# A one-layer hybrid encoder on one core: three products of a constant at the start, and a planner that runs eight passes

## The chip, the cores and the metric

The kernel runs on one core of a Trainium2 chip. The time is device microseconds of one execution; the median of 3 runs of the kernel before is 2115.37 us (2114.18 to 2116.24). A difference of about 0.2% (4.2 us) is what is treated here as a change.

## The reference, cut to what matters

One layer of a streaming encoder on 1024 frames of width 1024, all in float32, with a final norm:

```
h = rmsnorm(x);  proj = h @ w_in                 # 11 groups of columns
A: gated DeltaNet (conv + SiLU, l2 norm, chunked triangular solve, scan over chunks)
B: gated linear attention (low-rank forget gate, scan over chunks)
x += (sigmoid(a) * (o_a @ w_a) + sigmoid(b) * (o_b @ w_b)) @ w_out
x += cross attention of rmsnorm(x) over 256 memory tokens (4 heads)
x += square(relu(rmsnorm(x) @ w1)) @ w2
return rmsnorm(x)
```

The first matrix work on the chip is the keys and values of the memory tokens (`wk`, `wv`), since it needs the least data.

## The kernel before

Every float32 product is made of three fast ones (`fp32r`): each operand is split into a high part (a copy on ScalarE, line 622, or line 736 for the memory tokens) and a low part (a difference, line 623 or 737), and `mm3` (lines 582, 584 and 586) multiplies high by high, high by low and low by high into one PSUM bank (`pd`, or `ps`). Weights are loaded by SP in pieces of 128x512 into `raw` tiles and split into `wop` (or `whi` and `wlo`) tiles. So TensorE needs, for each piece of weights, one load, one ScalarE row and one VectorE row. PSUM banks are emptied by ScalarE (lines 935, 1302, 1588) and VectorE (line 940).

The big projections use a seven-product scheme on 2x2 blocks: lines 1757 to 1765 form sums of weight blocks before they are split, in place in `raw`. `t`, `A0a`, `A1b`, `B0b`, `B1b` are operand tiles on the activations' side. Other names that come up: line 1275 is one tap of the convolution, line 1176 and line 654 a merge of three buffers and the transposes that read one of them, line 1437 fills `PF`, the inverted diagonal blocks of the triangular solve, with four copies of one quarter each, and line 1449 multiplies by them.

The order of the instructions is not the order of the code. The program is traced once, then a planner (`Plan`) lays it out and the program is built again in that order. The planner gives each instruction a duration out of a formula (`Op`), works out backwards when each must be done at the latest (`latest`), and then runs forward in time: each engine takes, of what is ready, the instruction with the earliest latest time (`forward`); TensorE takes the first in the program. Some sums and low parts may run on VectorE or on GpSimd (POOL); `forward` chooses for each. Latest times go back from where TensorE is expected to be. `make` repeats the two steps and keeps the layout that ends first by the planner's own account:

```
for _ in range(ROUNDS):
    start, order = self.forward(deps, self.latest(deps, at, max(at) + 5000))
    at, end = start, max(start)
    if best is None or end < best[0]:
        best = end, order, [o.eng for o in self.ops if o.flex], start
```

With `ROUNDS` 1, the expected times of TensorE's work (`at`) are a plain sum of the durations; from the second pass on they are those of the pass before, waits included. `apply` then ties each engine's instructions together in the order kept. On the chip each engine runs its queue strictly in that order, and SP issues its loads and stores so too.

The run starts with `consts`: an identity, a 128x16 tile `mhalf` filled with -0.5 (used as an exponent by POOL), a column of ones and two small loads. SP meanwhile loads the first pieces of `wk` and the memory tokens.

Of the kernel before, what the change touches and what calls it, by code (L numbers as in the profile page):

```python
# [18 lines left out]
P = 128  # L19
# [8 lines left out]
HALF = 512  # L28
# [13 lines left out]
SE = ((0, 0, 0, 0, 0, 0, 0, 0), (0, 1, 0, 1, 1, 1, 0, 1), (0, 1, 0, 1, 0, 1, 0, 0))  # L42
FJ = 12
KRAW = 4
LAYW = (("raw", 2048, 2), ("whi", 4096, 2), ("wlo", 4096, 2))
FF = ((24, 24), (24, 24))
HEAD = (0, 1, 2)
# [26 lines left out]
OUT = "out_0_dram"  # L74
HOLD, MARGIN = 0, 0
SOON = 0
ROUNDS, TOP, PAD, WINDOW, LOAD, HORIZON, LAND, RATE = 1, 228656, 128, 3413, 1283, 30000, 2600, 300
ISSUE = 400
HEADIN = ('in_memT_dram', 'in_wk_dram', 'in_wv_dram')

# [420 lines left out]
class Layer:  # L501
# [134 lines left out]
    def wpart(self, src, shape, lo_eng=None, lp=None, before=None, rp=None):  # L636

        raw = self.til(rp or self.wp, [P] + shape, "raw", bufs=RAWS if rp is None else KRAW)
        hi = self.til(self.wp, [P] + shape, "wop", F32R, bufs=RING)
# [60 lines left out]
    def consts(self):  # L700
        nc, a = self.nc, self.a
        cp = self.cp = self.pool(self.ctx, "const", "left")
        self.room(cp, 160)
        self.ident = self.til(cp, [P, P], "ident")
        make_identity(self.tc.nc, self.ident)
        self.mhalf = self.til(cp, [P, 16], "mhalf")
        nc.vector.memset(self.mhalf, -0.5)
        self.ones = self.til(cp, [P, 1], "ones")
        nc.vector.memset(self.ones, 1.0)
        cols = self.til(cp, [P, 56], "cols")  # L710
        nc.scalar.dma_start(cols, a["cols"])
        self.g_mix, self.g_x = cols[:, 0:8], cols[:, 8:16]
        self.g_mem, self.g_mlp = cols[:, 16:24], cols[:, 24:32]
        self.b_gate, self.g_fin = cols[:, 32:36], cols[:, 48:56]
        self.a_log, self.dt_bias = cols[:, 39:40], cols[:, 40:41]

        self.g_gdn, self.g_gla = cols[:, 36:37], cols[:, 37:39]
        self.convw = self.til(cp, [P, 24, 4], "convw")
        nc.sync.dma_start(self.convw, a["convw"])
        self.tm = self.til(cp, [P, NB, 2, GH], "tm")  # L720
        self.geg = self.til(cp, [P, NB, GH], "geg")
        self.gneg = self.til(cp, [P, NB, GH], "gneg")
# [846 lines left out]
    def phase_gdn(self, wp):  # L1569

        nc, a = self.nc, self.a
        with ExitStack() as ctx:
# [3 lines left out]
            self.lay(sp, LAYP)  # L1576
            self.lay(wp, LAYW)
            self.lay(sq, LAYQ)
# [891 lines left out]
```

## Time and profile before

| | |
|---|---|
| median of 3 runs | 2115.37 us |
| the profiled execution, its own time | 2115.5 us |
| its span in the profile | 2113.8 us |
| granted TensorE clock | 0.999 |
| TensorE matmul (PE), busy | 2091.5 us (99%), 10938 records |
| VectorE (DVE), busy | 1595.6 us (75%) |
| ScalarE (ACT), busy | 1208.1 us (57%) |
| GpSimd (POOL), busy | 152.2 us (7%) |
| moved by DMA | 329.57 MB, mean 156 GB/s |

The span is what lies between the first and the last instruction of the program; the execution takes 1.7 us more. PE's busy time counts overlapped matmuls once, so a short wait can hide inside it: two matmuls of 128x512 follow each other in 0.23 us while each row is 0.39 us long. In a row of the timeline the figures are the start in us, the duration in us, and in brackets the engine's idle time before it with what ended it; of a wait of n us the bracket shows what the overlap has left.

### The profile page before, as it was taken

The page shows a single profiled execution, that of the slowest core. Times are in us where ns is not written, and L with a number is a line of the kernel's source. Part 1 is how long each engine was busy: PE and PEld are TensorE (multiplying, and loading weights), DVE is VectorE, ACT ScalarE, POOL GpSimd, SP SyncE. Part 2 cuts the span into 40 slices and gives each one's busy share as a digit, 9 for nine tenths or more (in the row PEclk, how much of TensorE's full clock was granted, in tenths as well). Part 3 has the DMA queues.
Part 4 walks back from the last instruction along what each step waited for, and adds up shares of the span by engine and source line. Part 5 has one row for each costly group of instructions (what it writes and reads, how often), then busy time and mean ns, then how long its engine had stood idle before and what let it go on. Part 6 is the DMA issues. An engine that isn't in the chain of part 4 may idle for free. (4 is left out here: it accounts for less than half of the span.)

```text
span 2113.8 us, 30953 instructions
## 1 busy us (share of the span) xinstructions
PE 2091.5 (99%) x10938; PEld 1780.5 (84%) x10938; DVE 1595.6 (75%) x2830; ACT 1208.1 (57%) x2391; POOL 152.2 (7%) x174
## 2 busy tenths in 40 slices
PE   8999999999999999999999999999999999999998
PEld 8889887898888899889888888888788888888887
DVE  7858887948876888787569899469967567567855
ACT  7456666536646586765655456565755557444433
POOL 0000000001001223311000000000100000000000
PEclk9999999999999999999999999999999999999999
DMA  8322232312325444555586752226444446678852
GB/s 329 130 72 62 91 105 64 113 61 96 100 93 194 131 129 139 168 176 162 176 278 239 257 169 80 90 79 218 137 145 140 160 151 219 212 249 278 269 175 100
DMA packets 158363, 329.57 MB, mean 156 GB/s; under 512 B 17016, under 2 KB 25720, under 8 KB 158208
## 3 DMA queue, kind: packets, MB, share of 16 engines
q1 hardware_dynamic: 158064, 327.57, 47.1%
q8 instruction: 86, 1.41, 0.3%
q14 instruction: 69, 0.57, 0.1%
q10 hardware_dynamic: 144, 0.03, 0.0%
HBM read 227.36 MB, written 100.17 MB: 155 GB/s over the span
## 5 line engine op out<-in xcount | busy, mean ns | idle before, releaser
L622 ACT ACTIVATE wop<-raw 128x512 fp32r<-128x512 f32 (+1 forms) x520 | 336.6, 653 | 406.4 <-PE pd L586 179.5
L623 DVE TENSOR_TENSOR wop<-raw,wop 128x512 fp32r<-128x512 f32 (+1 forms) x494 | 347.3, 707 | 209.3 <-ACT wop L622 206.4
L582 PE MATMUL pd<-t,wop 128*128 128x512 f32 x332 | 130.4, 393 | 0.9 <-ACT t L622 0.9
L586 PE MATMUL pd<-t,wop 128*128 128x512 f32 x332 | 130.9, 394 | 0.0
L584 PE MATMUL pd<-t,wop 128*128 128x512 f32 x332 | 130.7, 394 | 0.0
L584 PE MATMUL pd<-A1b,wop 128*128 128x512 f32 x272 | 106.1, 390 | 0.0
L582 PE MATMUL pd<-A1b,wop 128*128 128x512 f32 x272 | 106.0, 390 | 0.0
L586 PE MATMUL pd<-A1b,wop 128*128 128x512 f32 x260 | 101.4, 390 | 1.4 <-DVE wop L623 1.4
L1275 DVE SCALAR_TENSOR_TENSOR dx<-dx,convw,dx 128x1023 f32<-128x1023 f32 (+2 forms) x72 | 90.3, 1277 | 2.2 <-ACT dx L1273 2.0
L582 PE MATMUL pd<-A1a,wop 128*128 128x512 f32 x208 | 81.6, 392 | 0.0
L584 PE MATMUL pd<-A1a,wop 128*128 128x512 f32 x208 | 81.5, 392 | 0.0
L586 PE MATMUL pd<-A1a,wop 128*128 128x512 f32 x196 | 76.7, 391 | 0.0
L582 PEld LDWEIGHTS pd<-t,wop 128*128 128x128 f32 x332 | 62.2, 188 | 14.5 <-ACT t L622 1.3
L584 PEld LDWEIGHTS pd<-t,wop 128*128 128x128 f32 x332 | 62.3, 188 | 13.2 <-DVE t L623 0.4
L586 PEld LDWEIGHTS pd<-t,wop 128*128 128x128 f32 x332 | 62.4, 188 | 12.8
L622 ACT ACTIVATE whi<-raw 128x512 fp32r<-128x512 f32 x70 | 43.0, 628 | 34.3 <-PE pd L584 15.2
L582 PEld LDWEIGHTS pd<-A1b,wop 128*128 128x128 f32 x272 | 51.1, 188 | 10.6 <-ACT wop L622 0.3
L584 PEld LDWEIGHTS pd<-A1b,wop 128*128 128x128 f32 x272 | 51.1, 188 | 10.4
L586 PEld LDWEIGHTS pd<-A1b,wop 128*128 128x128 f32 x260 | 48.8, 188 | 11.9 <-DVE wop L623 1.9
L623 DVE TENSOR_TENSOR wlo<-raw,whi 128x512 fp32r<-128x512 f32 x65 | 44.0, 685 | 17.7 <-ACT whi L622 17.7
L940 DVE TENSOR_TENSOR dx<-pd,dx 128x512 f32<-128x512 f32 x51 | 35.0, 687 | 16.9 <-PE pd L586 16.7
L582 PEld LDWEIGHTS pd<-A1a,wop 128*128 128x128 f32 x208 | 39.0, 188 | 8.3 <-ACT dx L935 0.3
(645 smaller groups left out, 6497.0 us busy)
## 6 DMA issues: line engine op xcount, KB each, us to landing
raw<-in_w_dram SPq DMA_DIRECT2D x120, 256.0 KB, 3.8
raw<-in_w_dram SPq DMA_DIRECT2D x32, 512.0 KB, 3.8
e<-ad SPq DMA_DIRECT2D x63, 256.0 KB, 4.7
ad<-q SPq DMA_DIRECT2D x45, 256.0 KB, 2.7
rawa<-ad SPq DMA_DIRECT2D x42, 256.0 KB, 4.6
A0b<-tgd SPq DMA_DIRECT2D x32, 256.0 KB, 5.2
ad<-acc SPq DMA_DIRECT2D x30, 256.0 KB, 2.3
ad<-u SPq DMA_DIRECT2D x30, 256.0 KB, 2.6
```

The source lines that it names most:

```text
L582: nc.tensor.matmul(out, lh, rh, start=first and i == 0, stop=False, skip_group_check=True)
L584: nc.tensor.matmul(out, lh, rl, start=False, stop=False, skip_group_check=True)
L586: nc.tensor.matmul(out, ll, rh, start=False, stop=last and i == n - 1, skip_group_check=True)
L622: nc.scalar.activation(hi, raw, AF.Copy)
L623: (lo_eng or nc.gpsimd).tensor_tensor(lo, raw, hi.bitcast(F32), SUB)
L940: nc.vector.tensor_tensor(o, pt, o, ADD)
L1275: self.nc.vector.scalar_tensor_tensor(y[:, d:], x[:, :T - d], cw[:, 3 - d:4 - d], y[:, d:], MUL, ADD)
```

## The change

Two edits. After `mhalf` is set, three products of it with itself (16 columns of weights, a moving operand of 512 columns made by repeating the tile, plain float32) go into a PSUM bank that nothing reads. And the planner makes eight passes in place of one and keeps the one that ends first by its own account.

```
+WARM = 3
...
-ROUNDS, TOP, PAD, WINDOW, LOAD, HORIZON, LAND, RATE = 1, 228656, 128, 3413, 1283, 30000, 2600, 300
+ROUNDS, TOP, PAD, WINDOW, LOAD, HORIZON, LAND, RATE = 8, 228656, 128, 3413, 1283, 30000, 2600, 300
...
         nc.vector.memset(self.mhalf, -0.5)
+        pt = self.pss()
+        half = self.mhalf.rearrange("p (a b) -> p a b", a=1).broadcast_to([P, HALF // 16, 16])
+        for _ in range(WARM):
+            nc.tensor.matmul(pt[:16], self.mhalf, half, start=True, stop=True)
         self.ones = self.til(cp, [P, 1], "ones")
```

The added line of constants moves all later lines down by one, and the four lines in `consts` those after them by four more: line 623 of the kernel before is line 624 after, line 1275 is line 1280. Every tile that is made after the added bank carries a number that is higher by 1 in its first part and by 4 in its last.

TensorE's order starts with the three products and is otherwise nearly the same row by row in its first units; the queues of the other engines are laid out anew from about 20 us on. Three places follow.

VectorE, at the end of the second group of projections (near 350 us in the trace of before). `wop_3456` is the low part of a piece of weights that TensorE waits for; the lines 1275 (1280 after) are taps of the convolution. Before:

```order
L1275 SCALAR_TENSOR_TENSOR dx_3390<-dx_3279,convw_194,dx_3390 128x1022
L1275 SCALAR_TENSOR_TENSOR dx_3410<-dx_3362,convw_194,dx_3410 128x1023
L1275 SCALAR_TENSOR_TENSOR dx_3390<-dx_3279,convw_194,dx_3390 128x1021
L1275 SCALAR_TENSOR_TENSOR dx_3410<-dx_3362,convw_194,dx_3410 128x1022
L623 TENSOR_TENSOR wop_3456<-raw_3345,wop_3456 128x512
L1275 SCALAR_TENSOR_TENSOR dx_3410<-dx_3362,convw_194,dx_3410 128x1021
L1760 TENSOR_TENSOR raw_3345<-raw_3346,raw_3345 128x4x128
L1077 SCALAR_TENSOR_TENSOR ex_3222<-ex_3214,ex_3222 128x1024
```

And after (`wop_3460` is the same piece):

```order
L1082 SCALAR_TENSOR_TENSOR ex_3226<-ex_3218,ex_3226 128x1024
L1280 SCALAR_TENSOR_TENSOR dx_3394<-dx_3283,convw_198,dx_3394 128x1023
L624 TENSOR_TENSOR wop_3460<-raw_3349,wop_3460 128x512
L1280 SCALAR_TENSOR_TENSOR dx_3394<-dx_3283,convw_198,dx_3394 128x1022
L1280 SCALAR_TENSOR_TENSOR dx_3414<-dx_3366,convw_198,dx_3414 128x1023
L1280 SCALAR_TENSOR_TENSOR dx_3394<-dx_3283,convw_198,dx_3394 128x1021
L1280 SCALAR_TENSOR_TENSOR dx_3414<-dx_3366,convw_198,dx_3414 128x1022
L1765 TENSOR_TENSOR raw_3349<-raw_3350,raw_3349 128x4x128
L1280 SCALAR_TENSOR_TENSOR dx_3414<-dx_3366,convw_198,dx_3414 128x1021
```

The low part stood behind four taps and stands ahead of them now; the long row of line 1077 (1082) moved ahead of both.

ScalarE, in the first unit of the triangular solve (near 735 us). `whi` are high parts of weights, `PF` the four copies of line 1437 (1442), `acc_...<-pd` evictions. Before:

```order
L622 ACTIVATE whi_7517<-raw_7519 128x512
L1302 ACTIVATE acc_7498<-pd_7471 128x512
L622 ACTIVATE whi_7517<-raw_7523 128x512
L1302 ACTIVATE acc_7514<-pd_7501 128x512
L622 ACTIVATE fold_7784<-raw_7782 128x512
L1437 ACTIVATE PF_6319<-X_6317 32x32x16 x4
L622 ACTIVATE whi_7787<-raw_7789 128x512
```

And after:

```order
L623 ACTIVATE whi_7521<-raw_7527 128x512
L623 ACTIVATE fold_7788<-raw_7786 128x512
L1307 ACTIVATE acc_7518<-pd_7505 128x512
L1569 ACTIVATE acc_7675<-pd_7531 128x512
L623 ACTIVATE whi_7791<-raw_7793 128x512
L623 ACTIVATE whi_7791<-raw_7797 128x512
L1442 ACTIVATE PF_6323<-X_6321 32x32x16 x3
L623 ACTIVATE whi_7821<-raw_7823 128x512
L1569 ACTIVATE acc_7783<-pd_7678 128x512
L1442 ACTIVATE PF_6323<-X_6321 32x32x16
```

Two more splits and an eviction stand ahead of the copies into `PF`, and a split and an eviction between the third copy and the fourth. On SP the load of the first of these `whi` pieces (`raw_7523` after) stands right behind two loads of 512 KB (`v`) that stood 24 and 20 rows ahead of it before.

POOL, from the output projection on (1250 to 1600 us). `u`, `raw`, `acc` are sums that `forward` may place on VectorE or on POOL. Before:

```order
L1757 TENSOR_TENSOR raw_12811<-raw_12811,raw_12812 128x4x128
L613 TENSOR_TENSOR rs_y_13287<-n_v_13285,mhalf_188 128x4
L613 TENSOR_TENSOR rs_y_13375<-n_v_13373,mhalf_188 128x4
L1711 TENSOR_TENSOR m_13923<-m_13923 128x512
L623 TENSOR_TENSOR B1b_14659<-q_14655,B1b_14659 128x512
L1762 TENSOR_TENSOR raw_15561<-raw_15561,raw_15560 128x4x128
L1757 TENSOR_TENSOR raw_15747<-raw_15747,raw_15748 128x4x128
```

And after:

```order
L1716 TENSOR_TENSOR u_12572<-u_12572,q_12305 128x512
L1762 TENSOR_TENSOR raw_12815<-raw_12815,raw_12816 128x4x128
L692 TENSOR_TENSOR acc_12619<-acc_12619,e_12728 128x512
L692 TENSOR_TENSOR acc_12619<-acc_12619,e_12979 128x512
L614 TENSOR_TENSOR rs_y_13291<-n_v_13289,mhalf_188 128x4
L614 TENSOR_TENSOR rs_y_13379<-n_v_13377,mhalf_188 128x4
L1762 TENSOR_TENSOR raw_14341<-raw_14341,raw_14342 128x4x128
L1765 TENSOR_TENSOR raw_14670<-raw_14671,raw_14670 128x4x128
L1767 TENSOR_TENSOR raw_15565<-raw_15565,raw_15564 128x4x128
L1762 TENSOR_TENSOR raw_15751<-raw_15751,raw_15752 128x4x128
L624 TENSOR_TENSOR wop_15737<-raw_15564,wop_15737 128x512
```

The low part of `B1b` left POOL for VectorE; where one large sum stood at the start of the stretch (the first row) there are four now, one behind the other, and in all of the stretch nine where there were five.

## The prediction

> **What bounds the kernel now.** I read the page's busy shares first, then the list of TensorE's waits, then the timeline around each wait.
>
> ```profile
> PE 2091.5 (99%) x10938; PEld 1780.5 (84%) x10938; DVE 1595.6 (75%) x2830; ACT 1208.1 (57%) x2391; POOL 152.2 (7%) x174
> PE pd L582 <- ACT mT L736: 6.2, 2, 5.5
> PE pd L582 <- ACT q L935: 1.9, 2, 1.7
> PE pd L586 <- DVE wlo L623: 1.8, 2, 1.2
> PE ps L654 <- DVE ex L1176: 1.6, 1, 1.6
> PE pd L586 <- DVE wop L623: 1.4, 1, 1.4
> PE pd L582 <- ACT t L622: 0.9, 1, 0.9
> PE ps L1369 <- DVE kdt L1345: 0.4, 1, 0.4
> 2105.69 0.39 PE L586 MATMUL ps<-wop,A1b 128*128 128x512 f32 x1
> 2110.78 0.33 SPq L2250 DMA_DIRECT2D out_dram<-B0b  x1
> ```
>
> TensorE is the bound. It idles 6.2 us before and among its first products, 8.0 us in eight shorter waits (1.9 + 1.8 + 1.6 + 1.4 + 0.9 + 0.4), and 8 us behind its last matmul, which the change leaves as they are. All that a new order can win is in those 14 us and in the pace of the start; what it can lose has no such limit.
>
> The start shows a second loss, in stretches of the windows view and two pairs of matmuls:
>
> ```profile
> 5.50:8.10 2.60, 1.96 (x7) 1.64 (x7) 1.58 (x3) 1.69 (x5) 0.00 (x0) 1.00 1.02 321
> 8.10:11.50 3.40, 3.32 (x15) 3.32 (x16) 3.31 (x8) 3.40 (x10) 0.00 (x0) 1.00 1.04 368
> 11.50:14.90 3.40, 3.40 (x30) 3.40 (x29) 3.30 (x7) 3.40 (x6) 0.00 (x0) 1.00 1.01 414
> 9.41 0.41 PE L582 MATMUL pd<-mT,wop 128*128 128x256 f32 x1
> 9.62 0.41 PE L584 MATMUL pd<-mT,wop 128*128 128x256 f32 x1
> 11.86 0.28 PE L582 MATMUL pd<-mT,wop 128*128 128x256 f32 x1
> 11.97 0.28 PE L584 MATMUL pd<-mT,wop 128*128 128x256 f32 x1
> ```
>
> The columns are stretch, length, busy time and count of PE, its weight loads, DVE, ACT and POOL, granted clock, DMA share, GB/s. Until about 11.5 us the same matmul of 128x256 comes every 0.21 us (9.41 to 9.62), afterwards every 0.11 to 0.12 (11.86 to 11.97): 15 in 3.40 us, then 30. The clock column says 1.00 in all three, so it does not show this; the pitch does. 22 matmuls (7 + 15) ran at the slow pace, at 0.09 us more each: 2.0 us.
>
> **The three products.**
>
> ```profile
> 0.92 0.07 DVE L707 MEMSET mhalf<- 128x16 f32 x1
> 5.54 0.80 PE L582 MATMUL pd<-mT,wop 128*128 128x256 f32 x2 [5.54 <-ACT mT L736]
> 26.69 0.60 PE L679 MATMUL ps<-ident,rs_o 128*128 128x128 f32 x4
> L679 PE MATMUL ps<-ident,rs_o x28: 270/275/275, 26.7 to 2099.5; 128*128 128x128 f32 x28
> ```
>
> They can start when `mhalf` is set, at about 1.1 us (0.92 + 0.07 and a handover), and TensorE has nothing else until 5.54. Nearest price: two plain float32 products of 128 columns are four records, 0.60 us in all with 0.275 for the last, so (0.60 - 0.275) / 3 = 0.11 a record and 0.22 for 128 columns. 512 columns are 0.87 us, three products 2.6; at the slow pace twice that, 5.2. So they end between 3.7 and 6.3 us and hold up the first real product by 0 to 0.8 us. In return the slow pace should end sooner. In the trace it ended 6.0 us after the first matmul, and 3.4 us after the only gap (8.18). Counted from 1.1 us that is between 4.5 and 7.1 us, so the real matmuls run fast from the first, or after some seven at 0.21. The gain lies between 2.0 and 0.6 (2.0 - 0.8 - 7 x 0.09); ScalarE and VectorE, busy 3.40 and 3.31 of 3.40 us from 8.1 us on, could take back part. I take **-1.8**, with 0.8 to the bad (delay without faster pace) as the other end. The cover is TensorE's empty 5.5 us; without it the price would be 2.6 to 5.2.
>
> The Trainium skill ("TensorE: Matmul & The Clock Gate", Part 1) has the array at half its clock until one window of about 3.4 us was busy, and lets the windows run freely, so the release falls one to two windows after sustained work begins. The trace agrees: 6.0 us after the first, 3.4 after the gap. By that rule the gain is anything between my two ends, another one in each run.
>
> **The new order, place by place.** First VectorE near 350 us:
>
> ```profile
> 350.96 4.86 DVE L1275 SCALAR_TENSOR_TENSOR dx<-dx,convw,dx 128x1022 f32<-128x1022 f32 x4
> 358.13 1.22 DVE L1077 SCALAR_TENSOR_TENSOR ex<-ex,ex 128x1024 f32<-128x1024 f32 x1
> 356.47 0.50 PE L586 MATMUL pd<-A1b,wop 128*128 128x512 f32 x1 [1.44 <-DVE wop L623]
> 360.60 2.47 PE L654 MATMUL ps<-ident,dx 128*128 128x128 f32 x16 [1.57 <-DVE ex L1176]
> ```
>
> The low part now stands ahead of the four taps (4.86 us), so the wait of 1.44 goes. But TensorE then reaches the transposes (line 654) earlier and waits there for VectorE, which has the same rows to do before line 1176; only what it did not do before can be won. Between -1.4 and 0; I take **-0.5**, since VectorE's rows follow without a gap and the second wait should grow.
>
> Next, ScalarE near 735 us:
>
> ```profile
> 733.98 0.63 ACT L622 ACTIVATE whi<-raw 128x512 fp32r<-128x512 f32 x1 [0.20 <-DMA raw<-in_w_gate_dram]
> 735.56 0.50 PE L586 MATMUL pd<-A0a,wlo 128*128 128x512 f32 x1 [1.18 <-DVE wlo L623]
> 734.72 0.60 ACT L1302 ACTIVATE acc<-pd 128x512 f32<-128x512 f32 x1
> 740.68 4.53 ACT L1437 ACTIVATE PF<-X 32x512 f32<-32x512 f32 x4 [0.40 <-DVE X L1431]
> 745.23 0.63 ACT L622 ACTIVATE whi<-raw 128x512 fp32r<-128x512 f32 x1
> raw<-in_w_gate_dram SPq DMA_DIRECT2D x2, 256.0 KB, 3.0
> dm<-gcd SPq DMA_DIRECT2D x2, 512.0 KB, 4.6
> ```
>
> The wait of 1.18 is for a piece of weights that landed late. In the new queue its load stands right behind two of 512 KB; a load of 512 KB takes 4.6 us to land where one of 256 KB takes 3.0, so up to 2 x 1.6 later, unless the two were issued long before. And the four `PF` copies (1.13 each), on which the products of line 1449 wait, now have two splits (0.63 each) ahead, and a split and an eviction (0.6 each) before the fourth: 1.2 to 2.5 later. Together 0 to +5; TensorE has other products to fill in. I take **+2.0**, the nearer row being a single pair of splits and half of the late load.
>
> The wait of 0.9 for `t`: its split stood behind an eviction and the split of another piece on ScalarE; in the new queue both come later. Between -0.9 and 0; **-0.9**.
>
> Last, POOL:
>
> ```profile
> 1485.11 7.01 POOL L623 TENSOR_TENSOR B1b<-q,B1b 128x512 fp32r<-128x512 f32 x1 [68.74 <-ACT B1b L622]
> 1492.15 0.60 ACT L935 ACTIVATE q<-pd 128x512 f32<-128x512 f32 x1 [3.13 <-POOL B1b L623]
> 1492.80 0.50 PE L582 MATMUL pd<-B0b,wop 128*128 128x512 f32 x1 [1.74 <-ACT q L935]
> 1262.55 3.82 POOL L1757 TENSOR_TENSOR raw<-raw,raw 128x512 f32<-128x512 f32 x1 [226.35 <-DMA raw<-in_w_out_dram]
> L623 POOL TENSOR_TENSOR wop<-raw,wop 128x512 fp32r<-128x512 f32 x5 | 6.9, 1394 | 133.1 <-ACT wop L622 133.1
> L623 DVE TENSOR_TENSOR wop<-raw,wop 128x512 fp32r<-128x512 f32 x479 | 329.0, 691 | 194.9 <-ACT wop L622 193.0 <-DMA ald<-u 1.3
> 1200.00:1300.00 100.00, 100.00 (x443) 82.81 (x442) 98.73 (x164) 53.51 (x92) 3.82 (x1) 1.00 0.47 149
> ```
>
> The low part of `B1b` took 7.01 us on POOL where five others took 1.39 each; an eviction waited for its tile, and TensorE 1.74 for the eviction. On VectorE it is one more row of 0.69: **-1.7** (-1.7 to -1). But the same planner puts four sums on POOL between 1250 and 1280 us, where VectorE is 98.73 of 100 us busy and the one sum that stood there took 3.82. The case of `B1b` shows how much is forgiven: 7.01 - 1.39 = 5.6 late gave 1.74 of waiting, so about 3.9 was covered. Four at 3.82 are 4 x 2.4 = 9.7 late if they follow each other, and VectorE is freed of four rows of 0.69 meanwhile. Between 0 and +6 (9.7 - 3.9); I take **+1.6**, one such wait, since the four are spread over nearly 30 us.
>
> The Trainium skill ("SBUF — State Buffer", Who interferes with whom) says that a VectorE instruction with two SBUF inputs and a GpSimd one that reads SBUF exclude each other, the later blocked until the first has finished. The trace disagrees with a block of one instruction: a VectorE row is 0.69, the excess 5.6. By the rule four sums would lose 4 x 0.69 = 2.8, under the cover, and this term would be 0.
>
> **The sum**, against the profiled execution's own 2115.5 us (span 2113.8 and 1.7 around it): -1.8 - 0.5 + 2.0 - 0.9 - 1.7 + 1.6 = -1.3, so 2114.2; that execution lies 0.1 above the median of 2115.37, so **2114.1**.
>
> **Rivals.** *Faster*: the new waits do not come, because TensorE has other products near 740 and POOL's sums stay short: 2115.4 - 2.0 - 1.4 - 0.9 - 1.7 = 2109.4. For it: eight passes aim the latest times at TensorE's real times. Against: what the planner prices is a POOL sum of fixed length, and 7.01 shows what that is worth. Chance 0.27.
>
> *Slower*: POOL. If two of the four sums take 7.01, they are 11.2 late, 7.3 over the cover; with the rest of the sum (-2.9) that is 2115.4 - 2.9 + 7.3 = 2119.8. Any loss over 2.9 beyond the cover makes the kernel slower, 7.1 by over 0.2%. For it: of the seven sums quoted above two were stretched, by 2.4 and 5.6. Against: the other five. Chance 0.17.
>
> *The products don't lift the pace*, as they load 16 of 128 columns: +0.8 in place of -1.8, 2116.7. Chance 0.12; nothing in the trace shows a narrow product at the slow pace.
>
> **How the numbers follow.** The forecast itself has 0.44. A measurement of this kernel can tell about 0.2% (4.2 us) from no change: below 2111.2 is faster, above 2119.6 slower. Same: 0.44 + 0.12 = 0.56; faster 0.27; slower 0.17. The range reaches from just under the fast rival, 2108.5, to the edge of the slow one, 2119.5.
>
> **What would show it.** Right: three rows of `mhalf` from 1.1 us, and 128x256 matmuls 0.12 apart before 8 us; no wait of line 623 near 350; a longer one near 740; `B1b` gone from POOL; no wait of TensorE between 1250 and 1300. Wrong: matmuls still 0.21 apart at 8 us; a PE wait over 3 us anywhere that none of these places explains; POOL rows over 5 us with a wait of TensorE behind them.

## The result and the profile after

The changed kernel takes 2118.97 us in the median of 15 runs (2117.0 to 2121.65), the kernel before 2115.37 (15 runs, 2113.51 to 2117.73): a ratio of 1.0019, interval 1.0012 to 1.0025. The forecast was 2114.1; the time lies inside its range, but on the other side of before: 3.6 us slower instead of 1.3 faster. That is less than the 4.2 us that are treated here as a change, but the interval does not reach 1. The profiled execution took 2119.72 us (span 2118.0).

The busy shares and the list of TensorE's waits, after:

```profile
PE 2097.8 (99%) x10944; PEld 1782.4 (84%) x10944; DVE 1604.7 (76%) x2836; ACT 1223.2 (58%) x2403; POOL 154.3 (7%) x168
PE pd L587 <- DVE wlo L624: 3.2, 3, 2.4
PE ps L655 <- DVE ex L1181: 2.2, 1, 2.2
PE ps L1454 <- ACT PF L1442: 2.1, 1, 2.1
PE ps L655 <- ACT dx L1048: 1.4, 1, 1.4
PE ps L712 <- DVE ones L714: 1.0, 1, 1.0
PE pd L585 <- DVE wop L624: 1.0, 1, 1.0
```

The waits for `q` at 1493 and for `t` are gone, as forecast, and of the pair near 350 one wait of 2.2 (`ex`) is left; 2.4 for `wlo` (before 1.2), 2.1 for `PF` and 1.4 for `dx` are new. The list does not add up to the loss, so the table below takes TensorE's products one by one. Products are numbered in TensorE's order, and each cell says by how many microseconds the product of that number starts later than in the trace of before. "After" stands for two executions of the same program (the second is an experiment below).

```
before, us   after   after again   what lies ahead of it
    16.2     -1.29     -0.96       the head
   250.0     -1.18     -0.85
   265.4     +0.30     +0.62       transposes of dx at 262
   372.0     +0.24     -0.42       the pair of waits near 350
   674.9     +1.18     +0.52
   685.3     +0.17     -0.49       a wait for kdt in before
   759.1     +5.52     +4.50       ScalarE near 735, PF and X
  1101.2     +6.61     +4.15
  1107.4     +5.16     +2.70       the wait for t
  1316.1     +6.84     +4.22       POOL's sums
  1485.0     +6.69     +4.07
  1497.2     +4.16     +1.55       B1b
  2105.7     +4.22     +1.59       the last product
```

Near 675 and from 756 to 829 us TensorE's orders of before and after differ, so that a number stands for different products and the cells there are good to some tenths. One stretch of 75 us, from 685 to 759, costs 5.0 to 5.4 us, more than the whole loss. The other places are worth 1 to 2.5 each, of both signs. Between the two executions the steps at 262, 735, 1102, 1316 and 1490 agree to 0.4 us; of the 2.6 us by which their ends differ, 2.1 lie elsewhere (part of it in the section on the hardware). The step at 681 says nothing of the change: the wait of 0.38 for `kdt` there stands in that one trace of before, and the products alone, with the same order, do not have it.

The head first, as TensorE's timeline and as one stretch of the windows view (columns as in the prediction):

```profile
1.01 5.04 PE L712 MATMUL ps<-mhalf 128*16 128x512 f32 x6 [1.01 <-DVE ones L714]
5.98 0.50 PE L583 MATMUL pd<-mT,wop 128*128 128x256 f32 x2
6.30:8.00 1.70, 1.70 (x15) 1.56 (x13) 1.59 (x4) 1.70 (x5) 0.00 (x0) 1.00 1.03 340
```

The three products (six records) run from 1.01 to 6.05 at the slow pace and hold up the first real one by 0.44. From 6.3 us the 128x256 products come 15 in 1.70 us, the fast pace, which before reached between 11.5 and 11.7.

Now the stretch at 735 to 757, on TensorE, ScalarE and VectorE; the first TensorE row is that of before at the same products:

```profile
744.53 3.71 PE L1449 MATMUL ps<-PF,NT 128*128 128x96 f32 x32
...
736.74 0.50 PE L587 MATMUL pd<-A0a,wlo 128*128 128x512 f32 x1 [2.41 <-DVE wlo L624]
751.44 5.41 PE L1454 MATMUL ps<-PF,NT 128*128 128x96 f32 x32 [2.14 <-ACT PF L1442]
748.02 3.28 ACT L1442 ACTIVATE PF<-X 32x512 f32<-32x512 f32 x3 [1.71 <-DVE X L1436]
733.12 1.22 DVE L1476 TENSOR_TENSOR v<-v,vs 128x1024 f32<-128x1024 f32 x1
734.56 1.22 DVE L1476 TENSOR_TENSOR v<-v,vs 128x1024 f32<-128x1024 f32 x1
743.93 0.19 DVE L1432 TENSOR_TENSOR Pm<-Pm,pr 128x31 f32<-128x31 f32 x1
```

The `PF` copies waited for nothing on their own engine: ScalarE sat idle 1.71 us for `X`. `X` is the end of the triangular solve, a chain of 62 short dependent rows on VectorE (lines 1430 and 1432) and two transposes behind them, whose last short row stood at 737.21 in before and stands at 743.93 now. The new order puts wide rows between its steps, two sums of `v` (1.22 us each) among them. The same two sums hold up the first wait: the high part of that piece was ready at 732.92 (ScalarE), and its low part ran behind them, at 736.00. TensorE then loses twice: 2.14 us of waiting, and 1.70 us because the products behind the wait take 5.41 us instead of 3.71. The windows view shows the second loss directly:

```profile
753.36:756.56 3.20, 3.20 (x16) 3.20 (x16) 0.00 (x0) 2.06 (x5) 1.05 (x3) 0.50 0.57 189
756.56:759.50 2.94, 2.94 (x36) 2.94 (x36) 1.66 (x3) 2.56 (x6) 0.30 (x1) 1.00 0.00 0
```

For 3.20 us the granted clock is 0.50 and 16 products pass; then it is 1.00 again.

### The profile page after: what moved, and what is told of

The parts are those of the page before. It is cut to its first block, busy times and chain, and to the rows that moved or that the text cites. A ratio compares the mean times of both kernels' runs of the same rounds, so it can differ in the third digit from the quotient of the medians.

```text
span 2118.0 us, 30982 instructions
## 1 busy us (share of the span) xinstructions
PE 2097.8 (99%) x10944; PEld 1782.4 (84%) x10944; DVE 1604.7 (76%) x2836; ACT 1223.2 (58%) x2403; POOL 154.3 (7%) x168
## 4 chain that ended last, share of the span: by engine, by line
PE 82%; DVE 10%; DMA 3%; issue 2%; ACT 2%; SPq 1%; POOL 0%; DVEq 0%; ACTq 0%; POOLq 0%
PE pd L587 19%; PE pd L585 19%; PE pd L583 19%; PE ps L585 5%; PE ps L587 5%; PE ps L583 5%; PE ps L655 2%; DVE wop L624 2%; PE ps L1463 2%; DVE dx L1280 1%; PE ps L1454 1%; PE ps L1499 1%; PE ps L1148 1%; PE ps L1516 1%; PE ps L1150 1%
## 5 line engine op out<-in xcount | busy, mean ns | idle before, releaser
L583 PEld LDWEIGHTS pd<-A1a,wop 128*128 128x128 f32 x208 | 39.1, 188 | 8.1
L585 PEld LDWEIGHTS pd<-A1a,wop 128*128 128x128 f32 x208 | 39.0, 188 | 8.1
```

The costliest lines, as they stand in the source:

```text
L583: nc.tensor.matmul(out, lh, rh, start=first and i == 0, stop=False, skip_group_check=True)
L585: nc.tensor.matmul(out, lh, rl, start=False, stop=False, skip_group_check=True)
```

## The experiments

For most of them the kernel plans twice, once as after does (plan a) and once as before does (plan b, one pass, without the products), and takes the order of every engine from one plan up to a time of that plan and from the other behind it. `EMIT` is the number of products of the constant that the kernel then issues. In these kernels lines stand 33 to 46 further down than in after.

```diff
+    for until, which in CUTS:
+        p = plans[which]
+        now = {k for k, t in p["start"].items() if t < until and k not in done}
+        for e, q in p["order"].items():
+            order[e] += [k for k in q if k in now]
+        done |= now
```

**The products alone.**

```diff
+EMIT, CUTS = 3, ((100000000, 'b'),)
```

> The order of before on every engine, and ahead of it on TensorE the three products of the constant; so the products without the new order. Theory (the products lift TensorE's pace about 3 us earlier, and what they gain stays only until the first wait on VectorE): between the 1.3 us that after was ahead at 9 us and about 0.3 us faster than before, because the taps at 262 are set by VectorE and not by TensorE: 2114.6 against 2115.4. Rival 1 (the head's gain lasts to the end): 2114.1 or less. Rival 2 (the products cost as much as they bring): 2115.4 or more.

2114.62 us against 2116.29 for before beside it, ratio 0.9996 (0.9987 to 1.0004): not told apart from no change by its time. Its trace is 1.04 us ahead at 16 us and still 1.04 ahead at 372 (2.00 at the end, 0.6 of it by the wait for `kdt` that it does not have), so the head's gain is not lost at 262: VectorE came along there (its four taps start at 256.86, in before at 257.91, in after at 258.19). The expectation that VectorE would swallow it was wrong for this order. That the gain is 1.0 and not 1.8 has a row:

```profile
8.19 0.39 PE L616 MATMUL pd<-mT,wop 128*128 128x256 f32 x1 [1.01 <-ACT mT L774]
```

At the fast pace TensorE is through the first operands by 7.2 us and waits for the next ones until 8.19; in before that wait ended at 8.18 too.

**The order alone.**

```diff
+EMIT, CUTS = 0, ((100000000, 'a'),)
```

> The order of after on every engine, without the three products (they were there while the order was made, and are left out of the kernel). Theory (the loss sits in the order, the products are worth up to 1.3 us): 2119.0 to 2120.3, between the time of after and 1.3 us above it. Rival (the products themselves cost, by the place in the ps buffers that they take or by what they do to the throttle later): under 2118, nearer to before.

2118.03 us, 1.7 over before (ratio 1.0008, 0.9999 to 1.0017): between the theory and the rival, and by the time alone not told apart from before. Its trace ends 4.09 behind before, after's 4.22: in the new order the products are worth nothing that these traces show. It is 0.85 ahead at 16 us without the products, since its pace lifts at 9.3 us instead of 11.7. That is not shown to be the order's doing: the kernel with the stretch as after (below), which has the order of before there and no products, lifts at 11.7 and is 0.42 ahead. The steps at 262 (from -0.80 to +0.68) and at 735 (from +0.50 to +6.09) stand here without any product: they belong to the order.

**The stretch of the solve, as before and as after.**

```diff
+EMIT, CUTS = 3, ((660000, 'a'), (790000, 'b'), (100000000, 'a'))   # as before
+EMIT, CUTS = 0, ((660000, 'b'), (790000, 'a'), (100000000, 'b'))   # as after
```

> After, with the products, but what its planner starts between 660 and 790 us stands on every engine in the order of before (about 665 to 800 us on the chip); ahead of it and behind it the order of after. Theory (the loss of after is one place: the triangular solve on VectorE is drawn out by sums put between its steps, and TensorE waits at 737 and 751 and falls back to half pace): the lag between 690 and 800 us, 4 to 5 us of it, goes and stays away: 2114 to 2115. Rival (the lag is made up or made again elsewhere, since the kernel's end is set by VectorE or ScalarE further on): 2118 to 2119, as after.

> Before, without the products, but what the planner starts between 660 and 790 us stands in the order of after; the rest is the order of before. Theory (one place): 4 to 5 us over before: 2119.4 to 2120.4, with waits at L624 wlo and L1442 PF near 735 and 750 and eight products of L1454 at half pace behind the longest of them. Rival (the stretch is only late because after arrives late and with other work still open): within 1 us of before, 2114.4 to 2116.4.

With the stretch as in before: 2113.08 us, ratio 0.9986 (0.9977 to 0.9995), faster than before. The lag stays at +0.04 at 685 and is -0.76 at 759; the solve ends and `X` is copied 8 us earlier, and neither the wait nor the half pace is there:

```profile
734.79 0.50 PE L620 MATMUL pd<-A0a,wlo 128*128 128x512 f32 x1 [0.42 <-DVE wlo L657]
743.77 3.71 PE L1487 MATMUL ps<-PF,NT 128*128 128x96 f32 x32
739.91 3.32 DVE L1476 COPY subPT<-X 32x512 f32<-32x512 f32 x4
```

So this one place is the loss, and nothing later makes it again; which of its rows does it, this run can't tell. The opposite kernel took 2131.22 us, far more than expected, and most of that is not the stretch: from 685 to 759 its lag grows by 4.5 us (-1.35 to +3.12), as it should, though with a wait for `PF` of only 0.92 and the half pace at 735, behind `wlo`. But at the seam behind it two orders meet that do not fit, and TensorE waits twice more and runs at half pace for 10 us.

```profile
801.75 1.09 PE L688 MATMUL ps<-ident,k 128*128 128x128 f32 x8 [2.71 <-DMA k<-gdk]
809.12 1.97 PE L688 MATMUL ps<-ident,k 128*128 128x128 f32 x8 [4.96 <-DVE v L1553]
```

**Two sums behind the solve.** After, with the two sums of `v` moved behind the last copy into `subPT`.

```diff
+MOVES = ((5618, 5192, 'vector'), (5620, 5618, 'vector'))   # v sums behind subPT<-X
```

> After, with one edit: the two sums v of L1476 (1.22 us each), which after has put between the steps of the triangular solve on VectorE at 733 and 734.6, stand behind the last copy into subPT, before any product reads them. Theory (the solve is what the inverse at 751 waits for, and TensorE's fall to half pace comes from that wait): X is there 2.4 us earlier, the 2.1 us wait and the slow products (another 2 us) both go: about 2114.6, 2114 to 2115.5. Rival 1 (the wait goes but the half pace stays, since it comes from the 2.4 us wait for wlo at 737, which this edit leaves): 2116.5 to 2117. Rival 2 (ScalarE or the loads are as late as VectorE there): 2118 to 2119.

2117.49 us (ratio 1.0008, 0.9999 to 1.0017), 1.5 under after; neither theory nor rival, and the interval overlaps that of after. The wait that went was the other one: TensorE waits 0.40 for `wlo` at 734 instead of 2.41, gets 2 us ahead, and then stands before `PF` as long as ever, though `X` came 2.8 us earlier (0.6 of that is a lead which the chain had at its start; the two sums of 2.44 us in all make the other 2.2).

```profile
748.66 5.41 PE L1496 MATMUL ps<-PF,NT 128*128 128x96 f32 x32 [2.11 <-ACT PF L1484]
749.12:752.32 3.20, 3.20 (x16) 3.20 (x16) 2.81 (x4) 2.30 (x5) 1.77 (x2) 0.50 0.52 164
```

The sums had held up both the low part of the weights and the solve. The half pace follows the wait for `PF`: the wait for `wlo` is nearly gone here, and the 3.20 us at 0.50 are still there.

**Work in the wait.** After, with two more products of the constant right ahead of line 1454's first, into the tile that it overwrites.

```diff
+                for _ in range(2):
+                    nc.tensor.matmul(pt[:16], self.mhalf, self.half, start=True, stop=True)
             for i in range(4):
                 nc.tensor.matmul(pt[:, i * 96:(i + 1) * 96], NT[:, u + i, :], PF[:, v + i, 0:96], start=True, stop=True)
```

> After, with two further products of the constant (about 0.9 us each at full pace) issued on TensorE right ahead of the first product of L1454 at 751, into the tile that this product then overwrites; they need nothing that is late, so they run inside the 2.1 us wait. Theory (TensorE falls to half pace because it idles there): the wait for PF stays, the products of L1454 behind it run at 0.11 us a step instead of 0.21, and the run is about 2 us under after: 2116.5 to 2117.5. Rival (the pace falls for another reason, or the work of two products is too little to hold it): 2119 or up to 1 us more.

> The kernel with two products of the constant in the wait at 750 once more, one execution: its profiled execution took 2117.1 us, its eleven runs 2119.0 in the median. Theory (whether TensorE falls back differs from execution to execution): the products of L1454 at full pace again, and the extra time of a slower run at another place, as behind the wait at 360. Rival (the filler did nothing and the first trace was lucky): L1454 at half pace, 0.21 us a step, as in after.

At its place it did what the theory says, in both executions: the products behind it take 3.78 and 3.81 us instead of 5.41, at a clock of 1.00.

```profile
747.87 1.89 PE L1497 MATMUL ps<-mhalf 128*16 128x512 f32 x4
750.20 3.78 PE L1500 MATMUL ps<-PF,NT 128*128 128x96 f32 x32 [0.44 <-ACT PF L1483]
750.20:753.80 3.60, 3.60 (x32) 3.60 (x33) 1.24 (x3) 3.53 (x7) 1.34 (x4) 1.00 0.59 162
```

The five traces with a wait of 1.85 to 2.14 us there and without the filler (after twice, the order alone, the two sums behind, the two POOL sums on VectorE) all have the half pace behind it. But the time did not follow: 2119.01 us, ratio 1.0016 (1.0008 to 1.0025), no faster than after. Against the second execution of after the first trace is 1.85 us ahead at 759, 0.5 at 1005 and nothing at 1600, and the second trace lost at 361 and 737 what it saved at 751 (below). So half the pace is lost because TensorE idles (the last section has how long); that filling one wait pays is not shown.

**POOL's sums.** After, with two of the four sums on VectorE, at the place of their planned start.

```diff
+MOVES = ((9878, 10056, 'vector'), (10158, 10002, 'vector'))   # u<-u,q and raw<-raw,raw off POOL
```

> After, with two of its four late sums on POOL (u<-u,q at 1246, 6.4 us there, and raw<-raw,raw at 1270, 4.4 us) done on VectorE instead, each at the place that the planner's start of it gives. Theory (the two drawn-out sums are what makes TensorE lose 1.2 us between 1250 and 1320, by the 0.98 us wait for wop at 1318.8): 1.2 us under after: 2117.5 to 2118. Rival (VectorE has no room there, and 1.3 us more on it delays the same wop): as after or up to 1.3 us over it: 2119 to 2120.3.

2119.93 us, ratio 1.0020 (1.0011 to 1.0028): not faster than after, so the rival. POOL's rows in after and TensorE's wait behind them, then TensorE's waits with the two sums on VectorE:

```profile
1246.14 6.41 POOL L1716 TENSOR_TENSOR u<-u,q 128x512 f32<-128x512 f32 x1 [203.99 <-DVE q L1710]
1270.30 4.41 POOL L1762 TENSOR_TENSOR raw<-raw,raw 128x512 f32<-128x512 f32 x1 [17.75 <-ACT wop L623]
1275.94 1.30 POOL L692 TENSOR_TENSOR acc<-acc,e 128x512 f32<-128x512 f32 x1 [1.23 <-ACT e L691]
1318.81 0.50 PE L585 MATMUL pd<-wop,B0a 128*128 128x512 f32 x1 [0.98 <-DVE wop L624]
...
1318.23 0.51 PE L625 MATMUL pd<-wop,B0a 128*128 128x512 f32 x1 [0.47 <-ACT wop L665]
1319.79 0.50 PE L627 MATMUL pd<-wop,B0a 128*128 128x512 f32 x1 [1.05 <-DVE wop L666]
```

Two of POOL's four sums were drawn out, to 6.41 and 4.41 where an undisturbed one takes 1.30, and TensorE did not wait for them: its first wait after 1240 is that at 1318. Without them the same `wop` is as late, and 0.47 more is lost ahead of it: from 1107 to 1316 the lag grows by 2.3 us instead of 1.7. That leaves the order of VectorE's rows there as the cause, which no run changes by itself.

**Other passes of the order maker.** After, with the order of its first or its last pass.

```diff
-            if best is None or end < best[0]:
+            if best is None or n == KEEP:   # 0, then 7
```

> The products and the planner as in after, but the order kept is that of its first pass (planned end 2113.8 us) instead of that of its fourth (2105.2). Theory A (differences between the planner's ends carry over to the chip): 8.6 us over after, about 2127.6. Theory B (they don't: the chip's time hangs on a few places that the planner misjudges, as the solve at 720 to 750, and the fourth pass was chosen by an end that says nothing of them): no more than 4 us from before, 2112 to 2120, and so perhaps under after.

> As the run before, with the order of the last pass (planned end 2105.9 us, 0.7 over that of after). Theory A: 2119.7, within 1 us of after. Theory B: anywhere from 2112 to 2123, and with another place or none at which TensorE waits over 2 us.

The first pass gave 2122.09 us (ratio 1.0031, 1.0019 to 1.0042), the last 2120.89 (1.0025, 1.0015 to 1.0035). The last pass's time fits theory B, but its waits over 2 us stand where those of after stand (358 and 735); the first pass fits neither theory (B had it at 2120 at most). The planner has the first pass 8.6 us over the fourth, the chip has it 3.1 over; the last is 0.7 over the fourth by plan and 1.9 on the chip, with waits of 3.1 for `wlo` and 2.2 for `ex`. By the medians the planner's ranking holds among these three, though their intervals overlap. But the order of before, planned at 2106.4 and so 1.2 worse than the fourth pass, is 3.6 better on the chip: there an end that was better by 1.2 us said nothing.

**After once more.**

> After once more, one execution, for what differs between two executions of one program: theory, the waits come at the same places and with the same lengths to 0.2 us, and what differs are the places at which TensorE runs at half pace behind a wait (at 361 and 753 in the first trace). Rival: the half pace stands at the same places each time, and the 4.6 us between the fastest and the slowest run are spread over the whole program.

2117.07 us, 2.65 less than the first execution, with TensorE's waits at the same places (2.42, 2.23 and 1.86 in place of 2.41, 2.23 and 2.14). Behind the wait at 360 the first trace ran at half pace, this one did not; at 751 both did. That fits the theory for 1.0 us of the difference, made between 265 and 372; 1.7 more is spread between 742 and 1101 and was not traced to a row. The wait for `PF` differs by 0.28, a little more than the theory allows.

**The faster version.** The products, the order of before up to 1330 us, and that of after behind it.

```diff
+EMIT, CUTS = 3, ((1330000, 'b'), (100000000, 'a'))
```

> The three products, the order of before for all that the planner starts up to 1330 us, and the order of after behind that, where the low part of B1b is on VectorE instead of POOL. Theory (the parts of the change add: the products alone were 1.05 us ahead of before from 16 us on in their trace, and after makes up 2.0 us at 1490): about 3 us under before: 2112 to 2113.5. Rival (what after gains at 1490 is only slack that its own lateness left, or the seam brings a wait of its own): 2114.5 or more.

2112.19 us, ratio 0.9984 (0.9976 to 0.9993): faster than both kernels, as forecast. At 1316 us its trace is 0.32 behind before, at 1497 it is 2.38 ahead; the step at 1490 is the 2.5 us that after shows at the same place. The lead of the products, 0.88 at 265, is gone in this trace by 372, where TensorE fell to half pace behind a wait of 1.54. So the trace shows the gain at `B1b`; that the parts add, the time fits and the trace does not show.

## Why the prediction was wrong

**The step that failed is the term for ScalarE near 735**, taken at +2.0. It measured +5.0 to +5.4, at and over the upper end of its bounds (0 to +5; its two parts, 3.2 and 2.5, add up to 5.7). The prediction asked what stands ahead of the `PF` copies on ScalarE and ahead of a load on SP, and priced two splits and half a load. The copies were late for the operand they read: `X`, at the end of VectorE's longest chain. Rows put between the steps of that chain had no price. The late load, the other part of the term, cost nothing: the split behind it was done 3.1 us before the low part began. The sentence "TensorE has other products to fill in" was wrong as well: the queue ran dry twice, and the second time the pace fell, which the forecast had priced at the start only. With 5.2 in place of 2.0 the same sum gives 2117.3.

**A place that the sum left out.** At 262 TensorE arrives early and stands 1.39 us before the transposes of `dx`, since VectorE's taps there are 0.28 us later than in before: a step of +1.5, and a further +0.9 between 372 and 675, not traced to a row. With these the sum is 2119.7; the measured 2119.0 is within its other errors, which fall on both sides.

**The products** (-1.8) lifted the pace as said, and the rival by which they do not is out. In all eleven traces with them the pace lifts between 3.8 and 6.3 us (the prediction had 4.5 to 7.1), in the three without at 9.3, 11.7 and 11.7. Their gain was put too high: about -1.0 in the order of before, since the faster TensorE meets ScalarE's copies of `mT`. And the head differs from execution to execution: at 16 us the eleven traces with the products are 0.5 to 1.5 us ahead of before's, 1.0 in the mean, and two without them 0.4 and 0.85. So an estimate of the products' own worth, out of the means of eleven and three traces, is 0.6 us. The Trainium skill ("TensorE: Matmul & The Clock Gate", Part 1) lets the gate's windows run freely, so that the lift comes at another time in each run; these traces agree.

**VectorE near 350** (-0.5): two waits became one of 2.23. From 265 to 372 the lag changes by -0.06 in one execution and -1.04 in the other, around the forecast; the worse of the two has 1.0 us of half pace behind the wait, which the forecast did not price. **The wait for `t`** (-0.9): -1.45 in both. **`B1b`** (-1.7): -2.5. These three were right in sign and mechanism.

**POOL** (+1.6): the lag grows by 1.5 to 1.7 there, so the number fits by luck: the reason does not. Two sums were drawn out as feared, all of it covered; the wait comes from VectorE's own order. The slower rival, two sums at 7.01 us beyond their cover, named the right side of before for a wrong cause.

Every sign that the prediction named for being right came (the early rows, the pitch before 8 us, no wait of line 623 near 350, a longer one near 740, `B1b` off POOL, no wait between 1250 and 1300), and none of the signs for being wrong (the longest new wait is 2.41 us). They asked where waits would be, and the error was how much one place costs.

## What to carry to other kernels

When an order changes, price a wait from the chain that feeds the last operand, on whichever engine it runs, and not from the queue of the engine that issues the copy; a chain of short dependent rows on a busy engine is the first thing to look at, because wide rows put between its steps delay its end nearly in full (2.2 us here for two rows of 1.22). A wait of 2 us on an otherwise busy TensorE can cost nearly twice its length, through the pace behind it (2.14 and 1.70 us here). A planner's gain that is smaller than its own error at one such chain (1.2 against 5 us here) is no gain: take the pieces that the traces show to work, and leave the rest as it was.

## What was not expected of the hardware

TensorE fell back to half pace in the middle of a kernel that keeps it 99% busy, in after behind waits of 2.1 and 2.2 us. The Trainium skill ("TensorE: Matmul & The Clock Gate", HAM oscillation — how this bites in real kernels) gives as its rule that no idle gap may exceed about 3.4 us. These waits are shorter and cost the pace all the same, and the measurement decides. Whether a given wait does it differs between executions. Here is the windows view of 356 to 363 us, around the same wait of 2.23 us, in the two executions of after (all engines, columns as in the prediction), and then that stretch in pieces of 3.41 us, two of the first execution and three of the second:

```profile
356.00:363.00 7.00, 4.75 (x25) 3.78 (x24) 6.46 (x10) 5.27 (x11) 3.08 (x2) 0.83 0.35 80
356.00:363.00 7.00, 4.60 (x26) 3.29 (x25) 6.78 (x11) 5.49 (x10) 3.08 (x2) 1.00 0.27 72
357.22:360.63 3.41, 1.16 (x8) 0.61 (x7) 3.41 (x6) 2.39 (x5) 1.90 (x2) 1.00 0.03 12
360.63:364.05 3.42, 3.42 (x15) 3.06 (x15) 2.88 (x7) 3.04 (x6) 1.18 (x1) 0.50 0.96 258
355.64:359.06 3.42, 2.32 (x11) 1.58 (x9) 3.42 (x5) 1.79 (x3) 0.39 (x1) 1.00 0.00 0
359.06:362.47 3.41, 2.17 (x16) 1.69 (x16) 3.40 (x6) 3.17 (x6) 2.68 (x2) 1.00 0.47 114
362.47:365.88 3.41, 3.36 (x16) 2.64 (x15) 3.16 (x8) 1.77 (x5) 0.00 (x0) 1.00 0.92 338
```

The pieces are not chosen freely. In each of the fourteen traces the changes of the granted clock lie whole multiples of 3.413 us apart (in after at 5.65, 360.63, 364.05, 753.17 and 756.58: 104, 105, 219 and 220 steps behind the first), and where this grid lies differs from execution to execution. In the first execution nearly all of the wait falls into one window, which is idle for 2.25 of 3.41 us, and the next window runs at 0.50. In the second the wait lies across a boundary, 1.1 and 1.2 us of idle time on its two sides, and the pace holds. It is so throughout: at full pace a window with 1.85 us or more of idle time was followed by half pace in all 14 cases, one with less than 1.5 in none; of twelve in between, two. So what counts in these traces is the idle time within one window of the grid, about half of it, and a fall costs up to 1.7 us, half of the next window. The filler's wait fits: its two products leave 0.44 us idle there. This was read from the traces afterwards; no run was made to test it.

The same page (Part 1) has the gate's windows run freely, and the grid, which starts elsewhere in each trace, agrees. One more point for reading the profile: behind these waits the clock column shows 0.50, while at the start of the kernel it says 1.00 through stretches whose pitch is twice the later one. The first entry of the clock in a trace stands where the pace lifts (11.69 us in before, 5.65 in after); ahead of it the column has nothing to go by.
